# Decoder layer on one core: separate buffer rings and queues for weights and w_ada, folded statistics in the first norm, w_ada steps spread through the output projection

## The chip, the cores and the metric

The kernel runs on one core of one Trainium2 chip. The metric is the time of one execution in device microseconds; the median of three runs of the kernel before is 1479.42 us (1477.63 to 1480.88). Engines: TensorE (PE; weight loads are PEld), VectorE (DVE), ScalarE (ACT), GpSimd (POOL), SyncE (SP). Transfers are issued from the queue of an engine; before the change nearly all come from SyncE's.

## The reference

One layer of a decoder: 256 tokens, width 2048, everything in float32.

```python
mod = silu(c) @ w_ada + b_ada                      # 2048 x 12288
shift1, scale1, gate1, shift2, scale2, gate2 = split(mod, 6)
u = x * (1 + scale1) + shift1
glu_in, q, k, v, gates = split(u @ w_in)           # 2048 x 9216
# A: GLU, causal depthwise conv (31 taps), LayerNorm, swish, @ w_conv_out
# B: causal softmax attention, 8 heads of 128, partial rotary, @ w_attn_out
y = (sigmoid(gA) * A + sigmoid(gB) * B) @ w_out    # 2048 x 2048
x = LN(alpha * x + (1 + gate1) * y)
u = x * (1 + scale2) + shift2
a, val = split(u @ w_up)                           # 2048 x 11264
y = (silu(depthwise_conv3(a)) * val) @ w_down      # 5632 x 2048
out = LN(alpha * x + (1 + gate2) * y)
```

With 256 keys there is one block only, so the block-sparse attention is plain causal attention.

## The kernel before

**Weight stream.** All weights are read once, in chunks of 128 rows by 1024 columns (512 KB), each by one transfer from SyncE's queue into a tile `wraw` (chunk, lines 380 to 399). ScalarE rounds a chunk to fp32r (`wh`, L393), VectorE forms the remainder (`wl`, L394). TensorE multiplies three times: weight's high part with the activation's high and low part, weight's low part with the activation's high part (L405 to L407, or L415 to L417 where tokens are on the output's partitions). One chunk is 24 matmuls of 256 columns. `group` (L419) runs over the chunks of one group of output columns and accumulates in PSUM banks.

**adaLN.** `mod` is not computed by TensorE: w_ada comes in 13 pieces of 1024 columns (the first two of 512), each in steps (`ada`, lines 168 to 213). A step loads 512 KB into a tile `araw` and VectorE adds it, times the column of silu(c), to the accumulator `acc` (L207; the first step of a piece is ScalarE's, L205). `araw` and `wraw` share the tag "raw" and so one ring of five buffers (L46, L185, L382), except in the first piece; w_ada's transfers are issued from SyncE's queue, between the weights (L190, L192). A finished piece is read out a few chunks later (`later`): TensorE transposes it (L223), ScalarE sums with an accumulating copy (L229) or, for `quick`, VectorE reduces (L225).

**Order.** The order of the program is written by hand with rates: each chunk lets `ada`, the background work (convolution, norms) and attention advance by an amount, and each step costs what it yields (1.15 for a w_ada step). `ada_until(n)` runs steps at once until n pieces are done. A scheduler then orders each engine's instructions, in the main by the order of the program; an instruction whose inputs and buffers are free may move ahead on its own engine. Pieces 1 to 5 make u, 6 and 7 gate1, 8 to 11 scale2 and shift2 (512 columns of each, 4 feature tiles), 12 and 13 gate2.

**The middle.** The output projection (lines 743 to 778) runs in groups of 8, 4 and 4 feature tiles. After each group x is updated (L759). The first norm's centre is estimated from two tiles (m0), and subtracted (L767 for the upper eight tiles, L735 for the lower). `stats` squares a tile on ScalarE (L728) and adds the tile and its square over the partitions on TensorE with a matrix of ones (L729, L730), tile by tile, into one PSUM bank; for the first eight tiles this is background work (`ln1_tiles`). At the end of the second group `ada_until(9)` runs, then the background is drained. In the last group the w_ada rate is 0.6, but no step runs there, since nine pieces are the cap. Then the norm follows (lines 801 to 812) and the up projection starts (`up_item`); its need for row k of w_up is that tile k is normalised and pieces k//4 + 8, at least nine, are done.

**Others.** The depthwise convolution (lines 514 to 536) multiplies on ScalarE into `pr` (L533) and adds on VectorE; its norm is lines 538 to 571. The rotary embedding moves rows with transfers from POOL's queue (lines 583 to 591). The vectors of the features are loaded from POOL's queue at the start (L119).

Of the kernel before, what the change touches and what calls it, by code (L numbers as in the profile page):

```python
# [33 lines left out]
def layer_kernel(ctx: ExitStack, tc: tile.TileContext, x, c, w_ada, b_ada, w_in, conv_dw_w, conv_dw_b,  # L34
# [44 lines left out]

# [1 line left out]
    ident = cst.tile([128, 128], F32, name="ident")  # L81
    rows = slot(13, [128, 6, 128], F32, "rows")
    nc.scalar.dma_start(rows[0:16, 0], c.rearrange("o (r p) -> (o r) p", p=128))
# [25 lines left out]
    nc.gpsimd.memset(ones, 1.0)  # L109
    mask = cst.tile([128, 256], F32, name="mask")  # L110
    ropec = cst.tile([128, 256], F32, name="ropec")
    ropes = cst.tile([128, 256], F32, name="ropes")
    rows2 = wk.tile([44, 128], F32, name="rows2", bufs=1)

    def load_vectors():
        prev = [i for i in traced() if i.engine == mybir.EngineType.SP][-1]

        def put(dst, src):
            nc.gpsimd.dma_start(dst, src)  # L119

        r0 = 0
        for ap, n in ((conv_dw_b, 8), (conv_ln_g, 8), (conv_ln_b, 8), (b_conv_out, 16), (ln1_g, 16), (ln1_b, 16),
                      (ffn_dw_b, 44)):
            put(rows[r0:r0 + n, 2], vec(ap))
            r0 += n
# [5 lines left out]
        put(rows2, fwr[88:])  # L131
        put(mask, k_mask)
        put(ropec, k_rope[0])
        put(ropes, k_rope[1])

# [1 line left out]
    xT = wide(0, F32, "xT")  # L137
# [19 lines left out]

# [1 line left out]
    mod = cst.tile([128, 96], F32, name="mod")  # L159
# [6 lines left out]
    cap = [9]  # L166

    def ada(cols, done, n=None):
        n = n or 1024 // len(cols)
# [10 lines left out]
        for k0 in range(0, KT, m):  # L180
            if piece < EA:
                raw = slot((8, 9, 10, 12, 14, 15)[spare[0] % 6], [128, 1024], F32, "araw")
                spare[0] += 1
            else:
                raw = st.tile([128, 1024], F32, tag="raw", name="araw")  # L185
            for j in range(m):
                src = w_ada[(k0 + j) * 128:(k0 + j + 1) * 128]
                if len(cols) == 2:
                    src = src[:, cols[0]:cols[0] + 4096].rearrange("p (a b) -> p a b", a=2)[:, :, :n]
                    nc.sync.dma_start(raw[:, j * w:(j + 1) * w].rearrange("p (a b) -> p a b", a=2), src)  # L190
# [24 lines left out]
    def to_columns(acc, cols, n, quick=False):  # L215
        w = n * len(cols)
        red = wk.tile([128, 8], F32, tag="red", name="red")
        junk = wk.tile([128, 128], F32, tag="junk", name="junk", bufs=1)
        for b in range(w // 512):
# [158 lines left out]

# [1 line left out]
    def chunk(src, width, two=False):  # L380
# [61 lines left out]

# [1 line left out]
    lin = slot(6, [128, 8, 256], F32, "lin")  # L444
# [63 lines left out]

# [1 line left out]
    cacc, chi = [None], []  # L510

    pr = wk.tile([128, 2, 2, 256], F32, name="pr", bufs=1)

    def conv(g):
        hc = hcs[0]
        if g == 0:
            cacc[0] = slot(16, [128, 8, 256], F32, "cacc")
# [20 lines left out]
    def conv_norm():  # L538
        a = cacc[0]
        pm = pst("pm")  # L540
# [29 lines left out]
        yield 5.6  # L570
        quiet[0] = False

# [1 line left out]
    rps = []  # L574
# [21 lines left out]
    def attention():  # L596
# [4 lines left out]
        def head(h):  # L601
# [4 lines left out]
            p = pp[:, h % 2]  # L606
            nc.vector.tensor_tensor(p[:, 0:128], s0, mask[:, 128:256], OP.add)
            nc.vector.tensor_tensor(p[:, 128:384], s1, mask, OP.add)
            mx = wk.tile([128, 6], F32, tag="mx", name="mx")
# [40 lines left out]

# [1 line left out]
    ra0 = 1.0  # L652
# [19 lines left out]
    for i, (g, k0, k1, ra, rb) in enumerate(items):  # L672
# [6 lines left out]
        if i == 12:  # L679
# [11 lines left out]
            p = pst("fw1_ps")  # L691
            nc.tensor.transpose(p[:, :44], rows2, ident[:44, :44])
            fw1 = cst.tile([128, 44], F32, name="fw1")
# [31 lines left out]
    def stats(t):  # L725
        d = xT[t // 8][:, t % 8]
        sq = wk.tile([128, 256], F32, tag="t", bufs=4, name="sq1")
        nc.scalar.activation(sq, d, AF.Square)  # L728
        nc.tensor.matmul(stat[0], ones, d, start=t == 0, stop=t == KT - 1, skip_group_check=True)  # L729
# [12 lines left out]
    rates["ada"] = 0.9  # L742
    cuts = (0, 8, 12, 16)
    for t0, t1 in zip(cuts, cuts[1:]):
        nt = t1 - t0
        if t1 == 16:
            rates["ada"] = 0.6
        banks = group(list(range(KT)), w_out[:, t0 * 128:t1 * 128], uk(mh), uk(ml), feat, tags="a" * (nt // 2),
# [12 lines left out]
        if t0 == 0:  # L761
# [19 lines left out]
    def norm(k, n, center):  # L781
# [38 lines left out]

# [1 line left out]
    NP = 7  # L822
# [5 lines left out]
    def up_need(k):  # L828
        normed_until(k)
        ada_until(max(NB, k // 4 + 8))  # L830

# [40 lines left out]

# [1 line left out]
    lrows = [slot(i, [128, D], F32, n) for i, n in ((14, "l2g"), (15, "l2b"))]  # L874
# [39 lines left out]
    nst = [0, 0]  # L914
    bst = [cst.tile([128, 4 if C2 == 1536 else 5, nc.vector.BN_STATS_DIM], F32, name=f"bst{t}") for t in range(2)]
    for g, (c0, c1) in enumerate(((0, 1024), (1024, C2), (C2, 2048))):
# [65 lines left out]
```

## Time and profile before

| | before |
|---|---|
| three runs, us | 1477.63, 1480.88, 1479.42 |
| median, us | 1479.42 |
| span of the profiled execution, us | 1477.4 |
| TensorE busy, us | 1417.7 |
| VectorE, ScalarE, GpSimd busy, us | 1108.8, 796.9, 27.7 |
| moved by transfers, MB | 358.5 |

The page gives the profiled execution's own time as its span, first to last instruction; the runs' times hold some 2 us more around it. Matmuls overlap, so that one lasts 0.28 us in a row though the next begins 0.12 us later; a count of instructions in a stretch tells more of TensorE than its busy time. L12 is line 12 of the kernel.

### The profile page before, as it was taken

Reading aid. Unit: us, or ns where it says so; the run is one execution under the profiler, and the core shown is the slowest. Engines: PE = TensorE matmul, PEld = TensorE weight load, DVE = VectorE, ACT = ScalarE, POOL = GpSimd, SP = SyncE. Lnnn points to the kernel's source line nnn. Section 1 sums busy time; section 2 is a strip of 40 time slices with the busy share of each in tenths; the row PEclk is TensorE's granted clock in tenths of the full one; section 3 lists DMA queues with packets and bytes.
Section 4 is the critical chain, followed back from the end, with each engine's and each line's share of the span. In section 5 each row is a group of like instructions: output and inputs, shape, how many; then the busy total and the mean of one; then the engine's idle time right before and its main releaser. Section 6 shows DMA issues by size and latency. Waiting matters only on the chain.

```text
span 1477.4 us, 26835 instructions
## 1 busy us (share of the span) xinstructions
PE 1417.7 (96%) x10691; PEld 1364.2 (92%) x10691; DVE 1108.8 (75%) x1398; ACT 796.9 (54%) x1250; POOL 27.7 (2%) x57
## 2 busy tenths in 40 slices
PE   4899999999999989998999999999999999999996
PEld 4889999989999989997999999999999998888886
DVE  6788888998989879896877767988765545446456
ACT  3546436669987655345545576555444444343342
POOL 2000000210000000000000000000000000000000
PEclk9999999999999999999999999999999999999998
DMA  9999899886567657987799977778776676655662
GB/s 310 328 302 334 299 339 310 256 280 209 175 194 222 210 173 254 310 297 226 242 307 315 323 248 218 240 246 254 238 217 183 180 224 215 193 172 173 189 202 100
DMA packets 154990, 358.53 MB, mean 243 GB/s; under 512 B 12172, under 2 KB 26466, under 8 KB 154608
## 3 DMA queue, kind: packets, MB, share of 16 engines
q1 hardware_dynamic: 152704, 352.37, 74.0%
q0 software_dynamic: 1872, 4.33, 0.9%
q8 instruction: 83, 1.36, 0.4%
q14 instruction: 43, 0.35, 0.1%
q10 hardware_dynamic: 288, 0.12, 0.0%
HBM read 353.10 MB, written 2.10 MB: 240 GB/s over the span
## 4 chain that ended last, share of the span: by engine, by line
PE 75%; DMA 13%; DVE 8%; issue 2%; ACT 2%; SPq 0%; DVEq 0%; ACTq 0%
DMA araw<-in_w_ada_dram 9%; PE acc0a L405 5%; PE acc0a L407 5%; PE acc0a L406 5%; PE acc1a L405 5%; PE acc1a L407 5%; PE acc1a L406 5%; PE acc2a L406 3%; PE acc2a L407 3%; PE acc2a L405 3%; PE acc3a L405 3%; PE acc3a L406 3%; PE acc3a L407 3%; DVE wl L394 3%; DVE acc L207 2%
## 5 line engine op out<-in xcount | busy, mean ns | idle before, releaser
L393 ACT CAST wh<-wraw 128x1024 fp32r<-128x1024 f32 (+1 forms) x483 | 496.7, 1030 | 559.5 <-PE acc3a L416 132.7
L394 DVE TENSOR_TENSOR wl<-wraw,wh 128x1024 fp32r<-128x1024 f32 (+1 forms) x483 | 577.1, 1198 | 252.1 <-ACT wh L393 248.1
L207 DVE SCALAR_TENSOR_TENSOR acc<-araw,ccol,acc 128x1024 f32<-128x1024 f32 (+1 forms) x182 | 225.4, 1238 | 84.3 <-DMA araw<-in_w_ada_dram 82.6
L405 PE MATMUL acc0a<-u2h,wh 128*128 128x256 f32 x352 | 99.3, 282 | 4.8 <-ACT u2h L325 4.8
L407 PE MATMUL acc0a<-u2h,wl 128*128 128x256 f32 x352 | 100.3, 285 | 3.1 <-DVE wl L394 3.1
L405 PE MATMUL acc1a<-u2h,wh 128*128 128x256 f32 x352 | 99.4, 283 | 0.0
L406 PE MATMUL acc0a<-u2l,wh 128*128 128x256 f32 x352 | 99.4, 282 | 0.0
L406 PE MATMUL acc1a<-u2l,wh 128*128 128x256 f32 x352 | 99.2, 282 | 0.0
L407 PE MATMUL acc1a<-u2h,wl 128*128 128x256 f32 x352 | 99.2, 282 | 0.0
L533 ACT ACTIVATE pr<-hc,cw 128x256 f32<-128x256 f32 x200 | 88.8, 500 | 11.7 <-DVE cacc L535 11.3
L405 PE MATMUL acc0a<-uh,wh 128*128 128x256 f32 x256 | 74.9, 292 | 7.1 <-ACT uh L242 7.1
L407 PE MATMUL acc0a<-uh,wl 128*128 128x256 f32 x256 | 74.5, 291 | 3.2 <-DVE wl L394 3.2
L406 PE MATMUL acc0a<-ul,wh 128*128 128x256 f32 x256 | 73.4, 287 | 1.6 <-DVE ul L243 1.6
L405 PE MATMUL acc2a<-uh,wh 128*128 128x256 f32 x256 | 73.1, 286 | 0.5 <-ACT gb L487 0.5
L406 PE MATMUL acc2a<-ul,wh 128*128 128x256 f32 x256 | 73.4, 287 | 0.0
L405 PE MATMUL acc1a<-uh,wh 128*128 128x256 f32 x256 | 73.3, 286 | 0.0
L407 PE MATMUL acc1a<-uh,wl 128*128 128x256 f32 x256 | 73.2, 286 | 0.0
L407 PE MATMUL acc2a<-uh,wl 128*128 128x256 f32 x256 | 73.2, 286 | 0.0
L406 PE MATMUL acc1a<-ul,wh 128*128 128x256 f32 x256 | 73.2, 286 | 0.0
L405 PE MATMUL acc3a<-uh,wh 128*128 128x256 f32 x256 | 73.2, 286 | 0.0
L407 PE MATMUL acc3a<-uh,wl 128*128 128x256 f32 x256 | 73.0, 285 | 0.0
L406 PE MATMUL acc3a<-ul,wh 128*128 128x256 f32 x256 | 72.9, 285 | 0.0
(438 smaller groups left out, 4349.8 us busy)
## 6 DMA issues: line engine op xcount, KB each, us to landing
araw<-in_w_ada_dram SPq DMA_DIRECT2D x176, 512.0 KB, 5.1
wraw<-in_w_up_dram SPq DMA_DIRECT2D x176, 512.0 KB, 4.8
wraw<-in_w_in_dram SPq DMA_DIRECT2D x144, 512.0 KB, 4.9
wraw<-in_w_down_dram SPq DMA_DIRECT2D x55, 512.0 KB, 4.5
wraw<-in_w_down_dram SPq DMA_DIRECT2D x44, 384.0 KB, 3.7
wraw<-in_w_out_dram SPq DMA_DIRECT2D x32, 512.0 KB, 5.5
araw<-in_w_ada_dram SPq DMA_DIRECT2D x32, 256.0 KB, 5.7
wraw<-in_w_attn_out_dram SPq DMA_DIRECT2D x16, 512.0 KB, 4.5
```

Source lines behind the costliest of these rows:

```text
L207: op = nc.vector.scalar_tensor_tensor(acc, r, ccol[:, k:k + 1], acc, OP.mult, OP.add)
L393: nc.scalar.copy(wh, raw)
L394: nc.vector.tensor_tensor(wl, raw, wh.bitcast(F32), OP.subtract)
L405: nc.tensor.matmul(o, wh[:, cs], ah, start=first and i % 2 == 0, stop=False, skip_group_check=True)
L406: nc.tensor.matmul(o, wh[:, cs], al, start=False, stop=False, skip_group_check=True)
L407: nc.tensor.matmul(o, wl[:, cs], ah, start=False, stop=last, skip_group_check=True)
L533: nc.scalar.activation(pr[:, k % 2, i], src, AF.Copy, scale=w)
```

## The change

- The pool of streamed tiles has four buffers of "raw" for weights alone; w_ada has a ring "araw" of three. All pieces but the first load from GpSimd's queue instead of SyncE's.
- The two accumulators are two tags, taken in turn. During the convolution and its norm one of the two holds the convolution's products (`pr`), and a new piece starts only when the piece before is read out.
- First norm: the centre is subtracted in two operations of four tiles; ScalarE squares four tiles at once; VectorE folds eight tiles into two (and four into two for the second group), and TensorE adds only these over the partitions.
- The target before the last group is 8 pieces instead of 9, and the rate of w_ada is not lowered in the last group. The ninth piece has to be done at the second row of w_up, is read out by VectorE (`quick`), and all read-outs of this kind have priority. At the end of the second group the background is drained first.
- Smaller: a mask of 128 columns (ScalarE copies the unmasked half), the read-out's unneeded output goes to PSUM, `rows2` and `bst` use storage of other tiles.

```diff
-    st = ctx.enter_context(tc.tile_pool(name="st", bufs=5))
+    st = ctx.enter_context(tc.tile_pool(name="st", bufs=4))
...
+    one, turn = [False], [0]
...
-        acc_all = wk.tile([128, 1024], F32, tag="acc", name="acc", bufs=2)
+        while one[0] and (later or gate2):
+            yield 0.5
+        turn[0] = turn[0] if one[0] else 1 - turn[0]
+        acc_all = wk.tile([128, 1024], F32, tag=f"acc{turn[0]}", name="acc", bufs=1)
...
-                raw = st.tile([128, 1024], F32, tag="raw", name="araw")
+                raw = st.tile([128, 1024], F32, tag="araw", name="araw", bufs=3)
+            eng = nc.sync if piece < EA else nc.gpsimd
...
-                    nc.sync.dma_start(raw[:, j * w:(j + 1) * w], src[:, cols[0]:cols[0] + n])
+                    eng.dma_start(raw[:, j * w:(j + 1) * w], src[:, cols[0]:cols[0] + n])
...
-                    nc.scalar.activation(junk, p[:, i * 128:(i + 1) * 128], AF.Copy, accum_out=red[:, j:j + 1])
+                    nc.scalar.activation(p[:, i * 128:(i + 1) * 128], p[:, i * 128:(i + 1) * 128], AF.Copy, accum_out=red[:, j:j + 1])
...
-        to_columns(acc, cols, n)
         k0 = (cols[0] - 3 * D) // 128
-        u2_cols(k0)
+        with tc.high_priority():
+            to_columns(acc, cols, n, k0 == 4)
+            u2_cols(k0)
...
+        if g == 0:
+            one[0] = True
+            prs.append(wk.tile([128, 2, 2, 256], F32, tag=f"acc{1 - turn[0]}", name="pr", bufs=1))
...
-        quiet[0] = False
+        quiet[0] = one[0] = False
...
-            nc.vector.tensor_tensor(p[:, 128:384], s1, mask, OP.add)
+            nc.scalar.copy(p[:, 128:256], s1[:, 0:128])
+            nc.vector.tensor_tensor(p[:, 256:384], s1[:, 128:256], mask, OP.add)
...
+    def halves(dst, src, n):
+        nc.vector.tensor_tensor(dst[:, :n], src[:, :n], src[:, n:2 * n], OP.add)
+
     def ln1_tiles():
-        for t in range(8):
-            nc.vector.tensor_tensor(xT[0][:, t], xT[0][:, t], m0, OP.subtract)
-            stats(t)
-            yield 0.34
+        sq, sm = slot(6, [128, 8, 256], F32, "sqw"), slot(16, [128, 8, 256], F32, "sm")
+        for h in (slice(0, 4), slice(4, 8)):
+            nc.vector.tensor_tensor(xT[0][:, h], xT[0][:, h], m0[:, None, :].to_broadcast([128, 4, 256]), OP.subtract)
+            nc.scalar.activation(sq[:, h], xT[0][:, h], AF.Square)
+            yield 0.6
+        for j, src in enumerate((xT[0], sq)):
+            s = sm[:, j * 4:j * 4 + 4]
+            halves(s, src, 4)
+            yield 0.5
+            halves(s, s, 2)
+            for i in range(2):
+                nc.tensor.matmul(stat[j], ones, s[:, i], start=j + i == 0, stop=False, skip_group_check=True)
+            yield 0.5
+
+    def ln1_four():
+        sq = slot(6, [128, 8, 256], F32, "sqf")
+        d = xT[1][:, 0:4]
+        nc.scalar.activation(sq[:, 0:4], d, AF.Square)
+        for j, src in enumerate((d, sq[:, 0:4])):
+            s = sq[:, 4 + j * 2:6 + j * 2]
+            halves(s, src, 2)
+            for i in range(2):
+                nc.tensor.matmul(stat[j], ones, s[:, i], start=False, stop=False, skip_group_check=True)
+        return sq[:, 0]
...
-    NB = 9
+    NB = 8
...
-        if t1 == 16:
-            rates["ada"] = 0.6
...
+        elif t0 == 8:
+            drain(bg_q)
+            sq = ln1_four()
+            nc.scalar.activation(lc[:, 0:1], sq[:, 0:1], AF.Sqrt)
+            ada_until(NB)
         else:
             for t in range(t0, t1):
-                sq = stats(t)
-        if t0 == 8:
-            nc.scalar.activation(lc[:, 0:1], sq[:, 0:1], AF.Sqrt)
-            ada_until(NB)
-            drain(bg_q)
+                stats(t)
...
-        ada_until(max(NB, k // 4 + 8))
+        ada_until(max(9 if k else NB, k // 4 + 8))
```

## Rows read from the trace of the kernel before

**Rows 1.** The page: busy time of TensorE, and GB/s in 40 slices.
```profile
PE 1417.7 (96%) x10691; PEld 1364.2 (92%) x10691; DVE 1108.8 (75%) x1398; ACT 796.9 (54%) x1250; POOL 27.7 (2%) x57
...
GB/s 310 328 302 334 299 339 310 256 280 209 175 194 222 210 173 254 310 297 226 242 307 315 323 248 218 240 246 254 238 217 183 180 224 215 193 172 173 189 202 100
```

**Rows 2.** Windows: PE, PEld, DVE, ACT, POOL busy us (xcount); clock, DMA share, GB/s.
```profile
24.00:60.00 36.00, 31.10 (x217) 30.70 (x218) 27.69 (x35) 22.22 (x35) 0.00 (x0) 0.92 0.92 311
60.00:200.00 140.00, 134.43 (x1060) 130.47 (x1059) 117.66 (x125) 68.00 (x93) 0.00 (x0) 1.00 0.92 316
...
280.00:310.00 30.00, 30.00 (x174) 26.57 (x174) 30.00 (x39) 17.30 (x26) 13.69 (x28) 1.00 0.94 295
...
515.00:540.00 25.00, 19.73 (x128) 18.88 (x127) 20.19 (x26) 16.82 (x25) 0.00 (x0) 0.86 0.54 170
...
628.00:668.00 40.00, 37.22 (x264) 34.47 (x262) 36.86 (x50) 17.30 (x40) 0.00 (x0) 1.00 0.87 299
668.00:703.00 35.00, 29.92 (x220) 29.00 (x220) 20.26 (x28) 17.63 (x37) 0.00 (x0) 0.95 0.67 208
703.00:730.00 27.00, 26.96 (x214) 26.82 (x214) 24.30 (x40) 17.62 (x27) 0.00 (x0) 0.94 0.74 234
730.00:850.00 120.00, 116.93 (x967) 115.92 (x966) 89.22 (x89) 60.89 (x92) 1.45 (x2) 1.00 0.93 315
850.00:1195.00 345.00, 345.00 (x2910) 345.00 (x2910) 251.13 (x343) 189.24 (x296) 1.68 (x3) 1.00 0.73 224
```

**Rows 3.** Waits, 24 to 280, then 730 to 850: total us, times, longest.
```profile
ACT wh L393 <- DMA wraw<-in_w_in_dram: 56.6, 32, 3.2
...
DVE acc L207 <- DMA araw<-in_w_ada_dram: 27.2, 24, 3.2
```

**Rows 4.** Timeline of SyncE queue, 640 to 700 us: start, us, transfer, count.
```profile
645.85 15.03 SPq L190 DMA_DIRECT2D araw<-in_w_ada_dram  x10
661.84 11.52 SPq L384 DMA_DIRECT2D wraw<-in_w_out_dram  x8
```

**Rows 5.** Timeline of TensorE, from 640.6 us: statistics of the first norm.
```profile
641.22 0.59 PE L729 MATMUL pms<-xT,ones 128*128 128x256 f32 x2
641.65 0.59 PE L730 MATMUL pms<-sq,ones 128*128 128x256 f32 x2
```

**Rows 6.** VectorE groups, 628 to 668 us: count, busy us, mean ns, idle.
```profile
L207 DVE SCALAR_TENSOR_TENSOR acc<-araw,ccol,acc 128x1024 f32<-128x1024 f32 x15 | 19.2, 1282 | 2.9 <-DMA araw<-in_w_ada_dram 2.7
...
L767 DVE TENSOR_TENSOR xT<-xT,ln 128x1024 f32<-128x1024 f32 x2 | 2.4, 1220 | 0.0
```

**Rows 7.** VectorE's groups, 500 to 545 us, columns as above.
```profile
L207 DVE SCALAR_TENSOR_TENSOR acc<-araw,ccol,acc 128x1024 f32<-128x1024 f32 x4 | 5.1, 1282 | 4.1 <-DMA araw<-in_w_ada_dram 4.1
L535 DVE TENSOR_TENSOR cacc<-cacc,pr 128x512 f32<-128x512 f32 x5 | 3.4, 687 | 0.0
```

**Rows 8.** Timeline of TensorE, 17 to 26 us.
```profile
18.74 2.14 PE L144 MATMUL px<-ident,xr 128*128 128x128 f32 x8 [11.93 <-DMA xr<-in_x_dram]
...
24.28 0.58 PE L405 MATMUL acc0a<-uh,wh 128*128 128x256 f32 x1 [2.26 <-ACT uh L242]
```

**Rows 9.** ScalarE's groups, 640 to 680 us.
```profile
L229 ACT ACTIVATE junk<-pa 128x128 f32<-128x128 f32 x16 | 4.4, 276 | 2.5 <-PE pa L223 2.2
```

**Rows 10.** Timeline of POOL: an issue of a transfer.
```profile
280.08 0.53 POOL L583 DMA_DIRECT2D rp<-q  x1 [269.84 <-DVE q L485]
```

**Rows 11.** Transfers: count, KB, median us to landing; then w_ada landing.
```profile
araw<-in_w_ada_dram SPq DMA_DIRECT2D x176, 512.0 KB, 5.1
...
acc<-in_b_ada_dram POOLq DMA_DIRECT2D x2, 4.0 KB, 3.6
...
rows<-in_c_dram ACTq DMA_DIRECT2D x1, 8.0 KB, 2.3
...
DMA to landing us min/median/max: 2.8/5.2/7.8
```

More of the change, by code (lines that the diff above doesn't have):

```diff
@@ L81, in layer_kernel @@
     ident = cst.tile([128, 128], F32, name="ident")
-    rows = slot(13, [128, 6, 128], F32, "rows")
+    rows = slot(13, [128, 7, 128], F32, "rows")
     nc.scalar.dma_start(rows[0:16, 0], c.rearrange("o (r p) -> (o r) p", p=128))
@@ L109, in layer_kernel @@
     nc.gpsimd.memset(ones, 1.0)
-    mask = cst.tile([128, 256], F32, name="mask")
+    mask = cst.tile([128, 128], F32, name="mask")
     ropec = cst.tile([128, 256], F32, name="ropec")
     ropes = cst.tile([128, 256], F32, name="ropes")
-    rows2 = wk.tile([44, 128], F32, name="rows2", bufs=1)
     def load_vectors():
@@ L130, in load_vectors @@
         put(rows[:88, 5], fwr[:88])
-        put(rows2, fwr[88:])
-        put(mask, k_mask)
+        put(rows[:44, 6], fwr[88:])
+        put(mask, k_mask[:, 128:])
         put(ropec, k_rope[0])
@@ L189, in ada @@
                     src = src[:, cols[0]:cols[0] + 4096].rearrange("p (a b) -> p a b", a=2)[:, :, :n]
-                    nc.sync.dma_start(raw[:, j * w:(j + 1) * w].rearrange("p (a b) -> p a b", a=2), src)
+                    eng.dma_start(raw[:, j * w:(j + 1) * w].rearrange("p (a b) -> p a b", a=2), src)
                 else:
-                    nc.sync.dma_start(raw[:, j * w:(j + 1) * w], src[:, cols[0]:cols[0] + n])
+                    eng.dma_start(raw[:, j * w:(j + 1) * w], src[:, cols[0]:cols[0] + n])
             for j in range(m):
@@ L217, in to_columns @@
         red = wk.tile([128, 8], F32, tag="red", name="red")
-        junk = wk.tile([128, 128], F32, tag="junk", name="junk", bufs=1)
         for b in range(w // 512):
@@ L510, in layer_kernel @@
     cacc, chi = [None], []
-    pr = wk.tile([128, 2, 2, 256], F32, name="pr", bufs=1)
+    prs = []
     def conv(g):
         hc = hcs[0]
+        if g == 0:
+            one[0] = True
+            prs.append(wk.tile([128, 2, 2, 256], F32, tag=f"acc{1 - turn[0]}", name="pr", bufs=1))
+        pr = prs[0]
         if g == 0:
@@ L538, in conv_norm @@
     def conv_norm():
-        a = cacc[0]
+        a, pr = cacc[0], prs[0]
         pm = pst("pm")
@@ L606, in head @@
             p = pp[:, h % 2]
-            nc.vector.tensor_tensor(p[:, 0:128], s0, mask[:, 128:256], OP.add)
-            nc.vector.tensor_tensor(p[:, 128:384], s1, mask, OP.add)
+            nc.vector.tensor_tensor(p[:, 0:128], s0, mask, OP.add)
+            nc.scalar.copy(p[:, 128:256], s1[:, 0:128])
+            nc.vector.tensor_tensor(p[:, 256:384], s1[:, 128:256], mask, OP.add)
             mx = wk.tile([128, 6], F32, tag="mx", name="mx")
@@ L691, in layer_kernel @@
             p = pst("fw1_ps")
-            nc.tensor.transpose(p[:, :44], rows2, ident[:44, :44])
+            nc.tensor.transpose(p[:, :44], rows[:44, 6], ident[:44, :44])
             fw1 = cst.tile([128, 44], F32, name="fw1")
@@ L728, in stats @@
         nc.scalar.activation(sq, d, AF.Square)
-        nc.tensor.matmul(stat[0], ones, d, start=t == 0, stop=t == KT - 1, skip_group_check=True)
+        nc.tensor.matmul(stat[0], ones, d, start=False, stop=t == KT - 1, skip_group_check=True)
         nc.tensor.matmul(stat[1], ones, sq, start=False, stop=t == KT - 1, skip_group_check=True)
         return sq
+    def halves(dst, src, n):
+        nc.vector.tensor_tensor(dst[:, :n], src[:, :n], src[:, n:2 * n], OP.add)
     def ln1_tiles():
-        for t in range(8):
-            nc.vector.tensor_tensor(xT[0][:, t], xT[0][:, t], m0, OP.subtract)
-            stats(t)
-            yield 0.34
+        sq, sm = slot(6, [128, 8, 256], F32, "sqw"), slot(16, [128, 8, 256], F32, "sm")
[21 more added lines that the diff above has]
+        return sq[:, 0]
     up_src = w_up.rearrange("k (a b) -> k a b", a=2)
-    NB = 9
+    NB = 8
     rates["bg"] = 0.5
@@ L914, in layer_kernel @@
     nst = [0, 0]
-    bst = [cst.tile([128, 4 if C2 == 1536 else 5, nc.vector.BN_STATS_DIM], F32, name=f"bst{t}") for t in range(2)]
+    bst = [bada[:, t * 30:t * 30 + 30].rearrange("p (a b) -> p a b", a=5) for t in range(2)]
     for g, (c0, c1) in enumerate(((0, 1024), (1024, C2), (C2, 2048))):
```

## The prediction

> **What bounds the kernel now.** I read the busy table first: TensorE is busy 1417.7 us of the span of 1477.4 [rows 1], so only some 60 us can be won by removing waits, and the question is where they lie. The windows show it [rows 2]. From 850 to 1195 us TensorE never idles and an instruction, nearly always a 256-column matmul, goes by every 345 / 2910 = 0.119 us; that is the pace to hold the other stretches against. Idle there: 4.9 us in 24 to 60, 5.6 in 60 to 200, 5.3 in 515 to 540, 2.8 in 628 to 668, 5.1 in 668 to 703, 3.1 in 730 to 850. After a longer gap the granted clock is down too (0.92, 0.86 and 0.95 as means of 24 to 60, 515 to 540 and 668 to 703). The rest lies in the first 24 us and behind 1460, which the change leaves alone but for the start. In 24 to 200 and in 730 to 850 the DMA engines are 0.92 to 0.93 busy, at 311 to 316 GB/s, while single slices reach 339 [rows 1]. Next the waits: from 24 to 280 ScalarE's cast waits for weights 32 times, 56.6 us, and in 730 to 850 VectorE waits 27.2 us for w_ada [rows 3]: two streams in one queue of SyncE and one ring of five buffers, each held up by the other. Last the queue: before the last third of the output projection SyncE issues ten w_ada transfers in a row, 645.85 to 660.88, and only then, at 661.84, the eight weight chunks that TensorE needs next [rows 4]. The step counts of the code say the same: ada_until(9) makes up exactly ten steps there.
>
> **Term 1, LayerNorm 1 in the output projection (628 to 668).** *TensorE:* each call of L729 or L730 is two matmuls and takes 641.65 - 641.22 = 0.43 us [rows 5]. The first twelve tiles cost 24 calls before, and 4 + 4 after: 16 x 0.43 = 6.9 us less. *VectorE:* it is busy 36.9 of the 40 us [rows 2], so it binds. By the code's yields 16 w_ada steps fall between the start of the second third and its end, 15 of them in this window [rows 6]; with the target of 8 pieces seven do. That takes off 8 x 1.28 = 10.2 us. Eight subtractions of 256 columns become two of 1024, which I cost at nothing. Added are the folds: by the row for 1024 columns (1.22) [rows 6] and for 512 (0.69) [rows 7], 2 x (1.22 + 0.69) for eight tiles and 2 x 0.69 for four, 5.2 us. VectorE's work falls to 36.9 - 10.2 + 5.2 = 31.9 us; TensorE's is 264 records less 48 of statistics and a dozen transposes, 204 x 0.119 = 24, plus 8 x 0.43 = 3.4 of statistics and some 1.5 of transposes, 29. I take 8 us off the 40; bounds 11 (TensorE binds) and 3 (the folds, now ahead of the next weight splits in the drain, come late).
>
> **Term 2, last third (668 to 703).** Six of the moved steps land here, 6 x 1.28 = 7.7 us on VectorE, which is busy only 20.3 of 35 [rows 2]; if that cover were gone it would be the price. The gap before the first weights closes, and with it the clock loss behind it; eight transposes leave. 2 us off, bounds 3 off and 1 on. The wait from the last statistic over square root and reciprocal to the first up-projection matmul is untouched.
>
> **Term 3, start of the up projection (703 to 730).** The other four steps come as one block at the second row of w_up, with the ninth piece's read-out: 4 x 1.28 plus two reductions of 512 columns at 0.69, 6.5 us, in front of the normalisation of tile 2 and of the fourth weight split. VectorE is busy 24.3 of 27 us here [rows 2], 2.7 us of slack; 3.8 must show, a little more for the order. 4.5 us on, bounds 0 and 6.5. Terms 1 to 3: -5.5.
>
> **Term 4, own rings in 730 to 850.** Four weight and three w_ada buffers instead of five for both, and a w_ada transfer that waits on POOL's queue blocks no weight. At most the idle 3.1 us and a little clock can return. 2.5 us off; bounds 4 off, 2 on (longer landings).
>
> **Term 5, own rings in the first 200 us.** At most the 10.5 us idle return. The waits that cause them are of both kinds, but the engines are 0.92 busy, so I take less than half, 4.5 off. Against it stands the start: nothing on POOL holds back the second piece, so its first three buffers, 1.5 MB, go out beside the first piece and x. The transposes of x wait until 18.74 us and the first matmul comes at 24.28 [rows 8]; 1.5 MB at the 311 GB/s of [rows 2] makes that 4.8 us late at worst, but the piece is then there when the gap at 50 us would have come. 1.5 us on. Together 3 off; bounds 10 off, 5 on.
>
> **Term 6, the convolution's norm (515 to 540).** VectorE stands 4.1 us for w_ada there, in front of the operations that end the gap [rows 7]. 2 us off, bounds 5 off and 0.
>
> **Term 7, attention.** ScalarE copies 128 columns more per head; the nearest row is L229, 0.28 us [rows 9]: 8 x 0.28 = 2.2, in a stretch where it is nearly full. 1 us on, bounds 0 and 2.2.
>
> **At nothing:** the masks, the row vectors and bst only share storage; the one accumulator during the convolution delays piece 6 by three chunks at a rate of 0.35, and no use is near; the read-out's output in PSUM keeps its instructions. The rope transfers share POOL's queue, but a w_ada step comes only every 1.15 / 0.35 = 3.3 chunks there, with three buffers of lead. The memsets of the gate rows wait on POOL and could hold w_ada of the same piece, due 40 chunks later.
>
> **POOL's queue.** An issue occupies POOL for 0.53 us at 280 us, in a window (280 to 310) in which VectorE is busy all 30 us [rows 10, 2]. Some 190 such issues (176 and the second piece's 16) [rows 11] hide. A 4 KB transfer from POOL lands in 3.6 us, an 8 KB one from ScalarE's queue in 2.3: I add 1.3 us to w_ada's median landing of 5.2 (longest 7.8) [rows 11].
> The Trainium skill, SBUF — State Buffer, in "The 'DVE blocks DMA' trap (SWDGE)", says that VectorE operations in a two-port mode lock GpSimd out while it writes descriptors, and advises the SP or ACT queue: that speaks against this change. The trace does not bear it out for what fills 280 to 310 (fp32 with two operands), since issues there stay at 0.5 us; by the rule each step could be late by one VectorE instruction, 1.2 us, where the sum has none.
>
> **Sum:** -8 - 2 + 4.5 - 2.5 - 3 - 2 + 1 = -12 us. The profiled span is 1477.4 and the median of the three runs 1479.4, 2 us above; I set the sum against the latter: 1467.4.
>
> **Rivals.**
> (a) *The own rings bring nothing:* the DMA engines are the limit at 0.92 busy, and what w_ada gains the weights lose. For: that share. Against: slices at 339 GB/s, and waits of both kinds in one stretch. Terms 4 to 6 vanish: -5.5 + 1 = -4.5, 1474.9.
> The Trainium skill, DMA: Bandwidth & Descriptors, "Issuing engines are not separate DMA queues", says that transfers of several engines run on the same 16 DMA engines and that issuing from more of them saves only the sequencer's time; by that rule this rival holds.
> (b) *Slower, because w_ada's ring of three is too short for POOL's longer landings.* A buffer is bound for landing + 0.5 + 1.28 us, and three give a step every third of it. In the first 71 steps one is due every 1.15 chunks of 24 x 0.119 = 2.87 us: 3.3 us. The ring holds up to a landing of 8.1 us, which is the point that decides; 6.5 is my estimate, 7.8 the longest seen. At 9 us a step takes 3.6, 63 steps lose 19 us, VectorE stands, and the splits queued behind it too. Then -12 + 3 + 2.5 + 19 = +12.5, 1491.9. For: two queues share the engines, so each landing stretches. Against: VectorE works in order, so w_ada's backlog limits itself.
> (c) *The folds take back what the statistics gave:* VectorE binds from 628 to 730 with 6.5 us more at its end; terms 1 to 3 come to nothing: 1472.9. For: 24.3 of 27 busy in term 3. Against: 14.7 us free in 668 to 703.
>
> **Chances.** Forecast 0.50 (own range 1458 to 1474), (a) 0.17, (b) 0.18, (c) 0.15. The range for 8 in 10 goes from 1456 (terms 1, 4 and 5 near their good bounds) to 1488, which takes in (a), (c) and half of (b). 0.2% is 3 us, about what a measurement here can tell. Faster: 0.48 + 0.11 + 0.12 = 0.71; slower: 0.19, nearly all (b); within 0.2%: 0.10.
>
> **What would show it.** SyncE's queue without w_ada behind the first piece, and no block of ten; half the records of the statistics lines, and no TensorE gap in 628 to 668; a gap of some 4 us soon after the first up-projection matmul; the first matmul at 25 to 29 us, the gap at 50 shorter; fewer waits of casts for weights. Landings over 8 us, with VectorE waiting for w_ada more than now, would mean (b) and make the prediction wrong; unchanged idle in 60 to 200 and 730 to 850 would mean (a).

## The result and the profile after: slower by 0.7%

| | before | after |
|---|---|---|
| median of 5 runs each on one chip, us | 1480.88 (1477.63 to 1484.77) | 1489.94 (1488.11 to 1491.75) |
| span of the profiled execution, us | 1477.4 | 1486.3 |

The ratio is 1.0066 [1.0045, 1.0087]. 1467.4 was predicted, with 1488 as the upper end and 0.19 for slower. From the page after, against [rows 1, 11]:

```profile
PE 1410.9 (95%) x10659; PEld 1358.9 (91%) x10659; DVE 1111.8 (75%) x1400; ACT 795.9 (54%) x1235; POOL 154.2 (10%) x249
...
araw<-in_w_ada_dram POOLq DMA_DIRECT2D x176, 512.0 KB, 6.0
```

TensorE does 32 instructions less and is busy 6.8 us less, as Term 1 wanted, and the span is 8.9 longer: 15.7 us of new waiting. To find it I count TensorE's instructions from the start to a set of times, for both kernels (busy us, count in brackets, granted clock, DMA share, GB/s). Before:

```profile
0.00:60.00 60.00, 35.03 (x231) 0.95 0.94 315
0.00:200.00 200.00, 169.46 (x1289) 0.98 0.93 316
0.00:280.00 280.00, 249.46 (x1955) 0.99 0.91 311
0.00:515.00 515.00, 484.46 (x3756) 0.99 0.82 269
0.00:530.00 530.00, 497.45 (x3847) 0.99 0.82 268
0.00:545.00 545.00, 509.19 (x3924) 0.99 0.80 263
0.00:640.00 640.00, 604.18 (x4709) 0.99 0.81 265
0.00:700.00 700.00, 658.54 (x5091) 0.99 0.81 265
0.00:730.00 730.00, 686.27 (x5308) 0.99 0.80 263
0.00:850.00 850.00, 803.21 (x6272) 0.99 0.82 270
```

After:

```profile
0.00:60.00 60.00, 29.47 (x210) 0.98 0.91 297
0.00:200.00 200.00, 165.99 (x1289) 0.98 0.92 320
0.00:280.00 280.00, 241.04 (x1896) 0.98 0.91 321
0.00:515.00 515.00, 475.25 (x3689) 0.99 0.81 272
0.00:530.00 530.00, 490.25 (x3798) 0.99 0.80 270
0.00:545.00 545.00, 504.13 (x3908) 0.99 0.79 265
0.00:640.00 640.00, 590.15 (x4608) 0.99 0.81 271
0.00:700.00 700.00, 646.95 (x5051) 0.99 0.79 264
0.00:730.00 730.00, 667.73 (x5174) 0.98 0.78 262
0.00:850.00 850.00, 787.73 (x6175) 0.98 0.81 273
```

The missing instructions times 0.119 us are TensorE's delay. At 280, for example, it is (1955 - 1896) x 0.119 = 7.0 us. From 700 on, 32 x 0.119 = 3.8 us come off, since the folds leave 32 matmuls out. The change of the delay from stage to stage is what each stage lost or won:

| stage, us | 0 to 200 | 200 to 280 | 280 to 515 | 515 to 545 | 545 to 640 | 640 to 700 | 700 to 730 | 730 to 850 | the rest |
|---|---|---|---|---|---|---|---|---|---|
| lost (+) or won (-), us | 0.0 | +7.0 | +1.0 | -6.1 | +10.1 | -11.0 | +11.1 | -4.4 | +1.2 |

"The rest" is what is left of the 8.9 us between the spans. Three stages lose much.

**Start, and 200 to 280.** The transposes of x wait 6 us longer than in [rows 8], since POOL issues six transfers of the second piece beside the first piece. TensorE, then POOL, from the timeline:

```profile
24.75 2.13 PE L143 MATMUL px<-ident,xr 128*128 128x128 f32 x8 [15.28 <-DMA xr<-in_x_dram]
...
30.29 0.58 PE L410 MATMUL acc0a<-uh,wh 128*128 128x256 f32 x1 [2.26 <-ACT uh L246]
```
```profile
1.29 4.46 POOL L195 DMA_DIRECT2D araw<-in_w_ada_dram  x6 [0.35 <-issue]
```

By 200 us the rings have won the late start back. Then comes a wait that the kernel before did not have; the waits from 60 to 280 (total us, times, longest):

```profile
ACT wh L398 <- PE acc3a L411: 73.2, 39, 4.6
...
PE acc0a L410 <- ACT uh L246: 9.1, 3, 4.9
...
ACT wh L398 <- DMA wraw<-in_w_in_dram: 6.7, 4, 2.8
```

Weights are there in time now: from 24 to 280 the casts' waits for them fell from 56.6 us [rows 3] to 8.3, and most of the casts wait for TensorE to free a buffer. So TensorE reaches the columns of u before the w_ada piece that makes them is read out, and waits 9.1 us for `uh`, 4.9 of them in one wait between 200 and 240, where its mean clock is 0.94.

**515 to 640.** Here a gain hides part of a loss. TensorE's waits from 530 to 640, the longest before and the longest after:

```profile
PE acc0a L405 <- ACT chi L242: 5.3, 1, 5.3
```
```profile
PE acc0a L412 <- DVE wl L399: 9.0, 8, 1.7
```

The kernel before waits 5.3 us for the convolution's norm (`chi`), and its mean clock from 530 to 545 is 0.77. The changed kernel has no such wait: the norm's reciprocal starts 2.5 us later than before (530.5 against 528.0), but TensorE is 8.0 us late by then. So 6.1 us of its delay are taken up here, and 1.9 are left at 545. By 640 it has lost another 10.1, with VectorE as what TensorE waits for. VectorE's two costliest groups from 530 to 640 after, and in the experiment `e4_lazy` (below), in which additions don't run ahead:

```profile
L399 DVE TENSOR_TENSOR wl<-wraw,wh 128x1024 fp32r<-128x1024 f32 x33 | 39.8, 1216 | 0.2 <-ACT wh L398 0.2
L212 DVE SCALAR_TENSOR_TENSOR acc<-araw,ccol,acc 128x1024 f32<-128x1024 f32 x26 | 33.3, 1280 | 13.4 <-DMA araw<-in_w_ada_dram 12.5 <-ACT acc L210 0.8
```
```profile
L399 DVE TENSOR_TENSOR wl<-wraw,wh 128x1024 fp32r<-128x1024 f32 x35 | 42.5, 1222 | 11.0 <-ACT wh L398 11.0
L212 DVE SCALAR_TENSOR_TENSOR acc<-araw,ccol,acc 128x1024 f32<-128x1024 f32 x15 | 19.3, 1284 | 2.2 <-DMA araw<-in_w_ada_dram 2.2
```

26 w_ada additions run here, against 19 before. With their own buffers they are free to move ahead of the program's order, and the scheduler put them there: by the orders of the two programs 132 additions stand ahead of the 191st weight split after, 119 before. On VectorE, which works in order, each then stands with its 1.28 us and its wait for the transfer in front of the next split. TensorE waits 9.0 us for `wl`. So the steps that were to run in the last third had all been run before it: from 640 to 703 us the changed kernel has no w_ada addition on VectorE.

**700 to 730.** In the 28 us behind the first u2 tile, before and after:

```profile
701.60:729.60 28.00, 27.33 (x213) 0.94 0.70 222
```
```profile
701.00:729.00 28.00, 19.77 (x115) 0.72 0.67 224
```

98 instructions are missing, 11.7 us, with the mean granted clock at 0.72. By these lines 7.6 us of it are idle time (8.2 against 0.7); the other 4.1 are an estimate of what the lower clock costs. VectorE, then ScalarE, from the timeline:

```profile
703.43 3.92 DVE L212 SCALAR_TENSOR_TENSOR acc<-araw,ccol,acc 128x1024 f32<-128x1024 f32 x3
709.33 1.28 DVE L212 SCALAR_TENSOR_TENSOR acc<-araw,ccol,acc 128x1024 f32<-128x1024 f32 x1 [1.98 <-DMA araw<-in_w_ada_dram]
710.53 0.75 DVE L815 TENSOR_TENSOR xT<-xT,ln 128x256 f32<-128x256 f32 x2
```
```profile
712.00 1.15 ACT L210 ACTIVATE acc<-araw,ccol 128x1024 f32<-128x1024 f32 x1 [3.91 <-DMA araw<-in_w_ada_dram]
713.05 1.03 ACT L398 CAST wh<-wraw 128x1024 fp32r<-128x1024 f32 x1
713.99 0.60 ACT L334 ACTIVATE u<-xT,ub,us 128x256 f32<-128x256 f32 x1
```

The block of four steps stands there as predicted. But only three fit the ring: the fourth transfer was issued late, and VectorE waits for it. Behind it ScalarE waits 3.9 us with the first step of the *next* piece, which is in no hurry, in front of the activation that the third tile of u2 needs. Most of that wait lies beside VectorE's: the tile is normalised at 711.3 and its activation starts at 713.99, so some 2.7 us are ScalarE's share.

### The profile page after: what moved, and what is told of

Same layout as the page of the kernel before. It is cut to its first block, busy times and chain, and to the rows that moved or that the text cites. A ratio compares the mean times of both kernels' runs of the same rounds, so it can differ in the third digit from the quotient of the medians.

```text
span 1486.3 us, 26777 instructions
## 1 busy us (share of the span) xinstructions
PE 1410.9 (95%) x10659; PEld 1358.9 (91%) x10659; DVE 1111.8 (75%) x1400; ACT 795.9 (54%) x1235; POOL 154.2 (10%) x249
## 4 chain that ended last, share of the span: by engine, by line
PE 67%; issue 21%; DMA 7%; DVE 3%; POOL 1%; ACT 0%; SPq 0%; POOLq 0%; DVEq 0%; ACTq 0%
DMA araw<-in_w_ada_dram 6%; PE acc0a L410 4%; PE acc0a L411 4%; PE acc0a L412 4%; PE acc1a L411 4%; PE acc1a L410 4%; PE acc1a L412 4%; PE acc2a L410 3%; PE acc2a L412 3%; PE acc2a L411 3%; PE acc3a L410 3%; PE acc3a L411 3%; PE acc3a L412 3%; PE acc2a L420 2%; PE acc2a L421 2%
## 5 line engine op out<-in xcount | busy, mean ns | idle before, releaser
L212 DVE SCALAR_TENSOR_TENSOR acc<-araw,ccol,acc 128x1024 f32<-128x1024 f32 (+1 forms) x182 | 224.7, 1235 | 38.1 <-DMA araw<-in_w_ada_dram 36.4
L195 POOL DMA_DIRECT2D araw<-in_w_ada_dram x128 | 92.6, 724 | 483.1 <-DVE acc L212 324.8
L410 PEld LDWEIGHTS acc0a<-u2h,wh 128*128 128x128 f32 x352 | 67.6, 192 | 8.8 <-ACT u2h L330 5.2
```

Of the source, the lines that this page charges most:

```text
L195: eng.dma_start(raw[:, j * w:(j + 1) * w].rearrange("p (a b) -> p a b", a=2), src)
L212: op = nc.vector.scalar_tensor_tensor(acc, r, ccol[:, k:k + 1], acc, OP.mult, OP.add)
L410: nc.tensor.matmul(o, wh[:, cs], ah, start=first and i % 2 == 0, stop=False, skip_group_check=True)
```

## Experiments

All ran with timed runs of the kernel before on the same chip. The chips differ from group to group (the median of the kernel before is 1480.9 for the e runs, 1481.6 for f, 1482.2 for g, 1481.2 for h), so across groups the ratios are compared. The delays are taken as above, in us behind the kernel before (minus: ahead), with the 3.8 us off at 850 where a kernel has the folds. The next to last column is the time at which the first u2 tile starts, in place of a delay at 700: some kernels have passed that tile by then and others have not. The records stand for the 28 us behind it. Profiles of kernels that share their early program (the change, e3, e4, g3, h2) differ by 2.9 us at 280: no smaller difference is read.

| kernel | median, us | ratio | at 200 | 280 | 530 | 545 | 640 | 850 | u2 tile at | records |
|---|---|---|---|---|---|---|---|---|---|---|
| before |  | 1 | 0 | 0 | 0 | 0 | 0 | 0 | 701.6 | 213 |
| after | 1489.9 | 1.0066 [1.0045, 1.0087] | 0.0 | 7.0 | 5.8 | 1.9 | 12.0 | 7.7 | 701.0 | 115 |
| e1 | 1479.7 | 0.9999 [0.9983, 1.0016] | -5.4 | 1.9 | 0.0 | 1.0 | 5.1 | -2.8 | 693.6 | 141 |
| e2 | 1477.7 | 0.9987 [0.9975, 0.9999] | -5.4 | 1.0 | 1.1 | -2.4 | 5.4 | -3.3 | 693.8 | 147 |
| e3 | 1488.2 | 1.0059 [1.0037, 1.0081] | 1.1 | 9.3 | 7.4 | 4.2 | 13.6 | 9.2 | 702.4 | 121 |
| e4 | 1476.1 | 0.9963 [0.9949, 0.9976] | 2.0 | 9.9 | 7.9 | 4.8 | 4.4 | -3.2 | 694.6 | 153 |
| f1 | 1472.5 | 0.9929 [0.9914, 0.9943] | -5.8 | 0.4 | -1.0 | -0.4 | 0.7 | -8.1 | 690.0 | 155 |
| f2 | 1486.2 | 1.0036 [1.0018, 1.0054] | -1.2 | -0.4 | 0.0 | -0.4 | -0.2 | 5.8 | 707.4 | 207 |
| f3 | 1484.6 | 1.0016 [1.0006, 1.0025] | 2.1 | 9.3 | 7.4 | 4.2 | 13.1 | 4.0 | 709.7 | 211 |
| f4 | 1470.2 | 0.9913 [0.9896, 0.9929] | -4.3 | 2.4 | 0.5 | 2.0 | 1.5 | -8.7 | 697.5 | 214 |
| g1 | 1524.3 | 1.0299 [1.0259, 1.0339] | 17.0 | 28.1 | 28.8 | 23.1 | 35.3 | 40.2 | 734.3 | 131 |
| g2 | 1510.6 | 1.0188 [1.0166, 1.0210] | 13.3 | 18.3 | 14.6 | 10.4 | 21.4 | 28.2 | 711.0 | 136 |
| g3 | 1483.4 | 1.0013 [1.0000, 1.0026] | -0.2 | 7.5 | 6.3 | 2.4 | 12.3 | 1.7 | 706.8 | 206 |
| g4 | 1521.2 | 1.0257 [1.0227, 1.0288] | 1.1 | 1.3 | 0.0 | 1.8 | 5.2 | 33.6 | 712.5 | 209 |
| h1 | 1470.6 | 0.9924 [0.9903, 0.9946] | -4.4 | 2.3 | 0.4 | 1.8 | 1.4 | -9.4 | 694.8 | 199 |
| h2 | 1487.6 | 1.0045 [1.0026, 1.0064] | 0.5 | 8.4 | 6.9 | 3.3 | 13.8 | 8.1 | 709.2 | 172 |

**e1: the second piece from SyncE's queue.**

```diff
-            eng = nc.sync if piece < EA else nc.gpsimd
+            eng = nc.sync if piece < 2 else nc.gpsimd
```

> The changed kernel, with the second piece of w_ada issued from SyncE's queue again (behind the first piece, x and the first weights); all else as changed. Theory (the start): in the changed kernel the first 1.5 MB of that piece go out from POOL's queue beside the first piece and x, and the first matmul comes 6 us late (30.3 instead of 24.3), of which some 2 us are still left at 530 us. Then the first matmul is back at 24 to 25 us and the time is 2 to 4 us under the changed kernel's 1489.9: 1486 to 1488. Rival (the first 240 us are bound by the bytes moved, so it does not matter what goes first): the first matmul is early, but later gaps grow by as much, and the time is within 1 us of 1489.9.

It took 10 us off, more than either held, and not by the early start alone. The counts show a lead over the changed kernel of 5.4 us at 200, 5.1 at 280 and 5.8 at 530, but of 0.9 at 545: this kernel waits 5.1 us for `chi`, as the one before does, and the changed kernel doesn't. (Other profiles of the late program, e3, g3 and h2, stand at 2.4 to 4.2 there, so 1 to 3 us of the lead are left.) Then it loses 4.1 us from 545 to 640 where the changed kernel loses 10.1, though the same 132 additions stand ahead; VectorE's waits for w_ada from 530 to 640 are 6.3 us instead of 12.5. Another 3 us (26 records) come at the up projection's start. Why an early start makes the early additions cheaper isn't shown.

**e2: all of w_ada from SyncE's queue, own rings kept.** The line above becomes `eng = nc.sync`.

> The changed kernel with all of w_ada issued from SyncE's queue, in rings of its own as changed. Theory (own rings let the scheduler run w_ada's steps ahead of their place, and that costs): the order on VectorE is the same as in the changed kernel but for single steps, so the stalls between 530 and 640 us (10 us idle) and at the start of the up projection (9 us idle) stay; only the start gains: 1485 to 1488. Rival (POOL's queue is what costs: landing of w_ada 6.0 us in the median against 5.1, and VectorE waiting in order for it): the stalls go, 1475 to 1479, like the kernel before.

The rival's time came, but not its mechanism. It runs within 2 us of e1, with all other pieces from POOL's queue there and from SyncE's here, and the loss from 200 to 280 is in both. The stalls did not go: from 545 to 640 it loses 7.8 us, and it has 147 records. The queue itself is worth no more than those 2 us; what POOL's costs is the second piece that nothing holds back.

**e3: the ninth piece only at its first reader, row 4.**

```diff
-        ada_until(max(9 if k else NB, k // 4 + 8))
+        ada_until(max(NB, k // 4 + 8))
```

> The changed kernel, where the ninth piece has to be done only at row 4 of w_up, whose tile is the first to need it, instead of row 1. Theory (a block of four steps and a read-out in front of tile 2 makes TensorE stand in 700 to 730, where it passed 123 records against 214 in 27 us before): the steps spread over rows 1 to 4, the gap in 700 to 730 shrinks from 9 us to 4 at most, 1481 to 1485. Rival (VectorE has too much to do in 700 to 740 in any order): the gap moves behind row 2, and the time stays within 2 us of 1489.9.

The rival held: 121 records instead of 115, and the time is within 2 us. The stall only moves, into one wait of 8.8 us that ends at 726.8.

**e4: w_ada additions held near the program's order** (at most eight instructions ahead of it on VectorE), from the eighth piece on.

```diff
-    LZ = 99
+    LZ = 7
```

> The changed kernel, in which VectorE's step of a piece from the eighth on may stand at most eight instructions ahead of its place in the program (the constant LZ from 99 to 7). The order on VectorE then has 118 instead of 132 additions ahead of the 191st weight split, and the rest lies in the last third of the output projection. Theory (steps run ahead wait in order for w_ada and hold the weight splits behind them): TensorE's idle in 530 to 640 falls from 10.1 us to 4 or less, VectorE's waits for w_ada there from 12.5 to under 5, 640 to 700 grows by 2 at most, 1480 to 1484. Rival (only the sum of VectorE's work counts, wherever it stands): what 530 to 640 gains 640 to 730 loses, within 2 us of 1489.9.

14 us off, more than expected. From 545 to 640 the delay stays (4.8 to 4.4) where the changed kernel's rises by 10.1, with 15 additions from 530 to 640 instead of 26 (the groups above). The block remains, with 153 records.

**f1: e1 and e4 together.**

> Both repairs at once: the second piece from SyncE's queue, and from the seventh piece on w_ada additions no longer ahead of the program's order on VectorE. Theory (two separate costs): the lazy kernel took 1476.1 us and still began 6 us late, 5 us late at the convolution's norm and 4 us late at the first update of x; if that start carries through, 1476 - 4 to 5 = 1471 to 1472. Rival (the stretch up to 200 us is bound by transfers, so that a late start is made up, and the 10 us of the SyncE variant came from the same steps between 530 and 640): 1475 to 1477, no gain on top.

The theory's time came, and 1472.5 beats both kernels. Beside e4 the early start is worth 5 us, at 545 (-0.4 against 4.8) as at 850. But the two costs are not separate: alone the repairs took off 10 and 14 us, together 17 and not 24 (by the ratios 20 and not 25). e1 had already saved part of what the early additions cost.

**f2: the folds alone, in the kernel before** (functions `stats`, `ln1_tiles`, `ln1_four` and the drain of the change, with `NB = 9`).

> The kernel before with the folded statistics alone (nine pieces, rates, one ring as before). Theory: VectorE binds between 628 and 668 us (36.9 of 40 us busy), the folds add 5.2 us to it and the larger subtractions give back 1, so that the fewer matmuls show little: 1478 to 1482. Rival, the prediction's own first term without the moved steps (TensorE's 16 calls of 0.43 us, 6.9 us): 1473 to 1475.

Slower by 5 us, worse than the theory. The second group ends 3 us earlier, but its last statistics wait for the fold, and the last third's weights for the block of ten. Waits from 640 to 703, and SyncE's queue:

```profile
PE acc0a L405 <- ACT wh L393: 7.3, 1, 7.3
...
PE pms L759 <- DVE sqf L734: 3.5, 1, 3.5
```
```profile
646.89 18.47 SPq L190 DMA_DIRECT2D araw<-in_w_ada_dram  x10
666.32 12.25 SPq L384 DMA_DIRECT2D wraw<-in_w_out_dram  x8
```

The block takes 18.5 us instead of 15.0 and the weights go out 4.5 us later than in [rows 4]: the folds stand on VectorE in front of the additions that free the buffers.

**f3: rings, queue and accumulators alone** (statistics, nine pieces, rates and read-out of before).

> The changed kernel with the statistics, the target of nine pieces, the rates and the read-out of before: rings, queue, accumulators and attention's mask alone. Theory (the loss comes from w_ada steps that run early on VectorE between 530 and 640, which the rings allow, and from the late start; the up projection's start is as before, since nine pieces are done): about 8 us lost by 640, 2 to 4 won between 640 and 700 (the block of ten is smaller) and 2 to 3 between 730 and 850: 1481 to 1484. Rival (the rings are harmless and the spreading of the steps makes the loss): the terms 4 to 7 of the prediction, -6.5 us, 1473 to 1476.

The theory's mechanism held, its time by 0.6 us not. The rings by themselves bring the late start, the wait for u and the early additions (13.1 us by 640). The first u2 tile comes 8.1 us late, with four additions in front of the last third instead of ten, and by 850 the delay is 4.0.

**f4: f1 with nine pieces as the target** (`NB = 9`).

> f1 with the target of nine pieces before the last third, so that no block of steps stands behind the second row of the up projection. Theory: the gap at the up projection's start (3 us more than before in the lazy kernel) closes, but the steps run as a block again before the last third, from their own ring and POOL's queue, where VectorE has 14.7 us free and the weights are not behind them: 2 to 3 us less than f1. Rival (the block costs before the last third what it cost behind the up projection's start): within 1 us of f1.

2.3 us by the medians, as the theory said. The intervals overlap, though each of its four times lies below f1's four. The traces don't show where it arises: the 59 records that f1 lacks against it come back at the up projection, 7.0 us, but the first u2 tile comes 7.5 us later, and the two spans differ by 0.3 us.

**g1, g2: the ring sizes,** two buffers for w_ada and five for weights, then four and three.

> The changed kernel with two buffers for w_ada and five for the weights, instead of three and four. From the reciprocal of the convolution's norm to the first update of x the changed kernel takes 109.4 us, the one before 100.4; in it VectorE waits 12.5 us for w_ada. Theory (that loss is mostly waiting: an addition ahead of its turn stands in VectorE's queue until its transfer has landed, and the ring is too short for such a row of steps): with two buffers the waits grow to over 15 us and the stretch to 110 us or more; 1490 to 1494. Rival (it is VectorE's time: each addition that is pulled ahead costs its 1.28 us): by the two programs' orders seven fewer additions stand ahead of the last weight splits of the stretch, so 100 to 103 us and 1481 to 1485.

> The same the other way: four buffers for w_ada, three for the weights. Theory (waiting): the waits for w_ada in the stretch fall under 6 us and the stretch to 103 to 106 us, though more additions are pulled ahead; 1484 to 1488, if the third weight buffer isn't missed elsewhere. Rival (VectorE's time): as many additions and earlier, so 109 us or more, 1490 or more.

Neither tells the two apart as I meant it, since both have lost 17.0 and 13.3 us by 200 already. There the short ring of each is seen. In g1 VectorE waits 46.4 us for w_ada from 60 to 280 (14.7 after), in g2 the casts 59.6 us for weights (6.7 after):

```profile
DVE acc L212 <- DMA araw<-in_w_ada_dram: 46.4, 32, 3.7
```
```profile
ACT wh L398 <- DMA wraw<-in_w_in_dram: 59.6, 33, 4.4
```

From 545 to 640 they lose 12.2 and 11.0, against 10.1 in the changed kernel (being late, they stand at an earlier place of the program there). Between the reciprocal of the convolution's norm and the first update of x VectorE waits 19.2 us for w_ada in g1, 2.9 in g2, and 12.5 after. e2 has 3.2 us of these waits, the same 132 additions ahead, and loses 7.8. So the loss does not follow these waits, which speaks for the additions' own time; but e1, with 6.3 us of waits and as many additions, loses 4.1, so what sets its size stays open.

**g3: the changed kernel with `NB = 9` alone.**

> The changed kernel with the target of nine pieces before the last third, nothing else. In the 28 us after the first u2 tile it has 115 records of TensorE where before had 213, and all kernels with nine pieces have 207 to 214. Theory: the 98 records (11.7 us) come back, and 3 to 6 us are paid before the last third (from f1 to f4 it was 7.5 us, but here the steps have largely been done by then): 1482 to 1486. Rival (the block costs the same in either place): 1487 to 1490.

The theory held: 91 of the 98 records return, and the first u2 tile comes 5.8 us later (706.8 against 701.0). So the target of 8 pieces, which was meant to win, is by itself a loss: 1.0013 with nine, 1.0066 with eight.

**g4: the lazy order in the kernel before** (`LZ = 7`).

> The kernel before with w_ada additions no longer ahead of the program's order from the seventh piece on: whether the lazy kernel's gain needs the change at all. Theory (with one ring and SyncE's queue no step gets ahead, so there is nothing to hold back; the counts of additions ahead of each weight split are the same): within 2 us of before. Rival (the lazy order is a gain by itself, whatever the rings): 4 us or more faster than before.

39 us slower: neither theory. Most of it comes behind 700 (6.5 us of delay then, 33.6 at 850). The reading, argued and not tried, is that in the shared ring an addition that is put off keeps a buffer that a weight needs. Waits of the casts from 730 to 1000, before and g4:

```profile
ACT wh L393 <- DMA wraw<-in_w_up_dram: 22.8, 12, 3.1
```
```profile
ACT wh L393 <- DMA wraw<-in_w_up_dram: 48.4, 24, 6.5
```

So the lazy order costs with the shared ring and pays with the rings of the change. Of the kernels with own rings only those with it are clearly faster than the one before (e4, f1, f4, h1; not f3, e1 and, at 0.9987, hardly e2). The own rings with the lazy order and without the folds were not tried.

**h1, h2: more steps in the last third,** by the rate, in f1 and in the changed kernel.

```diff
+        if t1 == 16:
+            rates["ada"] = 1.5
```

> f1 with the w_ada rate at 1.5 instead of 0.9 in the last third: by the rate 8 x 1.5 / 1.15 = 10 steps run there, 4 more than in f1, so no block stands behind the second row of the up projection. Theory (the block costs only because of its place; VectorE has idle time in the last third): the 58 records that f1 lacks in the 28 us after the first u2 tile against before (155 against 213, 6.9 us) come back and 1 to 2 us are paid earlier: 1466 to 1468. Rival (the steps cost VectorE's time wherever they stand, as with f4, where 6.3 us of some 8 were paid back before the norm): 1470 to 1473.

> The changed kernel with the w_ada rate at 1.5 in the last third, nothing else. Theory (as for h1; the changed kernel lacks 98 records after the first u2 tile, 11.7 us, and its VectorE has the most idle time in the last third): 9 to 11 us off, 1479 to 1481. Rival (as much is paid before the norm as with nine pieces as the target, where 5.8 us were): 1482 to 1486.

The rival held in h1; h2 lies above both, nearer to the rival. 44 and 57 records return behind the norm (5.2 and 6.8 us), but the first u2 tile comes 4.8 and 8.2 us later, of which about 2 and 3 had arisen before the output projection's first update. What is left is within 2 us of f1 and 2.3 us below the changed kernel. So about half or more of what the steps cost behind the norm is paid in front of it when they stand there. f1, f4 and h1 cannot be told apart by their intervals; f4 is the lowest with 0.9913.

## Why the prediction was wrong, step by step

**The step that failed first: where the steps run.** Terms 1 and 2 took the w_ada steps from the code's yields ("16 w_ada steps fall ..., seven do", "six of the moved steps land here"). The front part says that an instruction whose buffers are free may move ahead on its engine, and own rings free the buffers. I priced them as supply only, and the sum had no term from 540 to 628. Measured from 545 to 640: +10.1 us, of which the lazy order leaves nothing in e4 (-0.4) and 1.1 in f1. None of the six steps of Term 2 was left for the last third.

**Terms 1 and 2** say -10 for 628 to 703; 640 to 700 gave -11.0. That VectorE binds fits f2: without the steps' move the same folds cost 5 us, more than in rival (c), where they come to nothing. But the steps left for 545 to 640, which paid for it. Beside own rings the folds win nothing either: f3 and g3 differ by them, the rates and the read-out, and stand at 1.0016 and 1.0013. Nor do the terms' counts close: eight steps are taken off and ten put back.

**Term 3** was mis-sized: 4.5 predicted, 11.1 measured, over its bound of 6.5. I counted VectorE's 6.5 us against its slack. Not in the sum were the fourth transfer, which a ring of three cannot hold ready (2.0 us), ScalarE's first step of the next piece in front of tile 2, and the clock (0.72 over 28 us) behind the gaps. How the excess divides among them was not tried. g3 shows the whole: 91 records back when the block is gone from there.

**Term 4** is right in kind: -2.5 predicted, -4.4 measured, and every kernel with three and four buffers has 1003 or 1004 records in the 120 us that follow the 28 (except e3, whose stall falls into them: 996), where before has 967.

**Term 5** had both sizes wrong. The late start cost 5.1 to 5.8 us up to 530 (e1), not 1.5; the bound of 4.8 for it was the better number. Behind 545 it is 1 to 3 us (e1), or 5 beside the lazy order (f1 against e4). The rings did win 5 by 200 us, as the 4.5 said (e1). But the win was one of weights over w_ada: by 280 it was gone, as a wait for u, in every kernel with three w_ada and four weight buffers. The last tile of u, made by w_ada's fifth piece, came at 231.5 us before and at 231.7 in e1. The DMA share from 200 to 240 is 0.95 before, 1.00 after and 0.96 in e1. So up to 280 it comes out as rival (a) has it; in 730 to 850 it doesn't.

The Trainium skill, DMA: Bandwidth & Descriptors, "Issuing engines are not separate DMA queues", says that issuing from more engines saves only the sequencer's time. e1 against e2 agrees, 1479.7 and 1477.7: the second queue brings nothing measurable. The Trainium skill, SBUF — State Buffer, in "The 'DVE blocks DMA' trap (SWDGE)", spoke against the change. The trace does not bear it out for what VectorE runs here either (fp32 with two operands): the 128 issues last 0.72 to 0.85 us, and 28 of POOL's lie between 530 and 640, where VectorE is busy 94.7 of 110 us.

**Term 6** had the wrong cause. VectorE's 4.1 us of waiting for w_ada from 500 to 545 are gone in e1 and f1 as in the changed kernel, and still e1 and f1 wait 5.1 us for `chi`, where the kernel before waits 5.3. The changed kernel is free of that wait, and of 6.1 us of its delay, but there TensorE is 8.0 us late and the norm only 2.5; in e1 both are 2.1 late, and the wait is there. So the gain is luck, not the term. **Term 7** lies in 280 to 515, +1.0 as forecast, but it was not tried alone, and 1 us is less than two profiles differ by.

**Rival (b)** came nearest in time (1491.9) by another mechanism. w_ada's landing rose to 6.0 us only, and VectorE's waits for w_ada over the whole kernel fell from 82.6 to 36.4 us. With two buffers its sum holds up to a landing of 4.8 us; in g1 the median is 5.1, and VectorE waits for w_ada as above.

**Rival (c)** has the right kind for the folds without the moved steps (f2), not for the change as a whole.

The sum in short: -12 was forecast and +8.9 came. Of the 21 us between, Term 5 missed 10 (the start and the wait for u), the early additions, which had no term, are 10, the block at the up projection (Term 3) is 7 more than forecast and the rest 1; terms 1, 2, 4, 6 and 7 came out 7 better, most of it by the wait for `chi`. By kernels: f3, terms 4 to 7 alone, is 0.16% or 2.4 us slower where -6.5 stood, and from f3 to the whole change it is 7 us slower where terms 1 to 3 had -5.5.

## What to carry to other kernels

Where a scheduler may move instructions ahead, giving a stream its own buffers changes the order on every in-order engine that consumes it, not only its supply: count the instructions that stand ahead of the critical ones in both programs' orders, and hold the stream back by priority together with the ring. One edit can cost without another and pay beside it (the lazy order cost 39 us with the shared ring and won 14 with the own one), so each should be tried both ways. A delay can vanish where the kernel that is ahead has to wait anyway, so a cost read in one stage should be followed past the next such wait before it is counted (here 8.0 us at 515 and 1.9 at 545). A stall that another operand hides, here u behind the weights, should be looked for before a gain from faster supply is written down.

## What had not been expected of the hardware

An issue from POOL took nearly twice as long as from SyncE: 0.72 us (median of 128) for a transfer from two ranges of columns, 0.53 (median of 64) from one, against 0.38 and 0.33 on SyncE's queue before. POOL is busy 154.2 us with them instead of 27.7, and this costs nothing that e1 against e2 shows.
